# Sink column in the softmax, subtractions and sums moved to GpSimd, and three reordered places in a two-layer diffusion backbone

## The chip, the cores and the metric

The kernel runs on one core of one Trainium2 chip. The metric is device time in microseconds (us) of one execution; it is quoted as the median of several. Engines are named as in the profile: PE (TensorE matmul), PEld (its weight loads, beside PE), DVE (VectorE), ACT (ScalarE), POOL (GpSimd) and SP (SyncE, which here only issues DMAs).

## The reference

Two layers over 1024 latent tokens of width 1024, with a prefix of 256 context tokens. Layer 0 is windowed attention: 16 query heads, 4 key/value heads, head width 128. Each latent query sees the keys within 128 positions and all 256 context keys, in one softmax that also has a learned sink logit per head. Layer 1 is a convolution branch. Each branch has a SiLU gate; each layer adds gate × branch to the stream; a final RMSNorm ends it.

```python
# layer 0, per head, block of 128 queries
p = softmax(concat([sink, ctx scores, window scores (masked)]))   # the sink's own p is dropped
o = p_ctx @ v_ctx + p_win @ v_win
y = (o * silu(z)) @ w_out
# layer 1
a, gl, z = split(h @ w_in + b_in, 3)
u = depthwise_conv31(a * sigmoid(gl)) + dw_b
y = (silu(layernorm(u)) * silu(z)) @ w_out
# both: h = rmsnorm(x) * (1 + scale) + shift;  x += gate * y;  at the end rmsnorm(x, final_g)
```

## The kernel before, in words

Every product of the size of a layer is made of three matmuls. Each fp32 operand is split in a high part (type fp32r, a rounded copy, made by ACT) and a low part (full minus high, `split_lo`, a two-input subtraction on DVE or POOL); then high×high, high×low and low×high are summed in PSUM. SBUF is handed out as 45 pages of 128×1024 words and 6 half pages of 128×528.

The order of PE's instructions is the order of the program text; the other engines' orders are made by a planner that simulates the program, ready work of earlier text first. In a trace nearly all instructions carry line 88, that of a wrapper that records them, so they are told apart by the names of their tiles: `pss`, `psg` and `pso` are the three kinds of PSUM banks (`ps_s` two of 1024 columns, `ps_g` two of 512, `ps_o` two of 512).

The stages, in order of time:

1. **Start** (to about 100 us): modulation vectors, first norm, the first projections.
2. **Attention** (about 100 to 900 us). `steps` goes over 16 heads × 8 query blocks. One step issues on PE: `scores` of the *next* block (6 matmuls into an `s` bank), 12 matmuls of filler (`fill(FILL)`: the z and q projections of the next head, from a queue `fillq`), every fourth step a `pv` (probabilities × values), and the `transposes` of the *present* block's probabilities `p` (also into an `s` bank). Between the scores and the transposes of a block lies its softmax, on DVE, ACT and POOL: a masked copy with a running maximum (`mx`), a small DVE step that makes it `nmx` = min(−scale·mx, −sink), the Exp with its sum `l0`, a second small Exp for the sink (`es`), their sum, a reciprocal `ri`, and the scaling of `p` by POOL. The tile `sc` holds these five columns. After the transposes ACT makes `pthi` and DVE `ptlo` from the bank, which then is free.
   Beside these run: `rope` for q and k (two DMAs that swap halves, a product with cos on DVE, one with sin on POOL, their sum on DVE, a copy on ACT, a low part on POOL); `low_parts` (64 subtractions 128×512 on DVE that store the low parts of both output projections' weights to DRAM, `wolA` and `wolC`); and `ada_rest` (sums for the modulation vectors, on DVE, in `mask_page`). `after(...)` only orders an instruction behind an anchor on the same engine.
   In the last head the filler ends; from block `EARLY_FROM` the queue gets `early_proj`, which computes the first `EARLY_ROWS` row pairs of the output projection (two of their four token blocks each, 12 matmuls per row pair).
3. **Output projection of layer 0** (about 900 to 1074 us), `proj_attn`. Its last sub-block pushes eight `turn_in` jobs, which make the second token half of the input of layer 1 (`h2h`, `h2l`) and are taken up during the first chunks of `b_mm`.
4. **Convolution layer** (about 1074 to 1610 us). `b_mm(i, half)` multiplies weight chunk `i` with one token half. The first `2 * EARLY` = 4 chunks are run for half 0 and then again for half 1; all later ones do both halves in a row. DVE and POOL/ACT compute the 31 taps beside this; `layer_norm` follows on PE's fixed order, its mean taken from `vsum`.
5. **Output projection of layer 1** (from about 1610 us), `proj_out`. `evac1` adds the residual, sums squares, and for the second column half makes the root (`rstd_of`) and writes out the normed rows: one instruction per half that multiplies with the root `r` and the weight `fg` at once. The last three row pairs are held back so that the four token blocks end one after another.

Of the kernel before, what the change touches and what calls it, by code (L numbers as in the profile page):

```python
# [12 lines left out]
ALU = mybir.AluOpType  # L13
# [20 lines left out]
FILL = 12  # L34
DEFER = 6
EARLY = 2
EARLY_ROWS = 6
EARLY_FROM = 4
KEEP = 8
BYBLOCK = 3  # L40
ZV = (1, 4, 7)
# [52 lines left out]
def backbone_kernel(  # L94
# [428 lines left out]
               for t, n in (("dww", NJ * TAPS), ("wsum", NJ * 16))]  # L523

    anchor = []
    anchor_max = []

    def after(ins, anchor=anchor):
        if anchor:
# [50 lines left out]
    def low_parts():  # L580

        items = [(pair_rows(w, m, kk), d[m, kk]) for w, d in ((Wo, wolA), (Wp, wolC)) for m in range(2) for kk in range(NK)]
        for src, dst in items:
            raw = pg.alloc(F32, [2, 512], "low")
            SY.dma_start(out=raw, in_=src)
            yield "open"
            for b in range(2):
                hi = hp.alloc(F32R, None, "lhi")
                act(hi[:, 0:512], raw[:, b], AF.Copy)
                after(split_lo(V, raw[:, b], raw[:, b], hi[:, 0:512]), anchor_max)  # L590
                hp.free(hi)
                if b == 0:
                    yield "open"
            SY.dma_start(out=dst, in_=raw)
            pg.free(raw)
            yield "shut"
# [182 lines left out]
            PE.matmul(o, wl[:, kt], Hh[kt][:, sl], start=False, stop=kt == KT - 1)  # L779
            yield  # L780

    def rope(o, sl, dh, dl):
        qe, qs, m = (hp.alloc(F32, None, "rope") for _ in range(3))
        e, w, r = qe[:, 0:512], qs[:, 0:512], m[:, 0:512]
        act(e, o, AF.Copy)
        A.dma_start(out=w[0:64], in_=e[64:128])
        A.dma_start(out=w[64:128], in_=e[0:64])
        tt(V, r, o, cos[:, sl], ALU.mult)
        tt(G, w, w, sin[:, sl], ALU.mult)
        tt(V, r, r, w, ALU.add)  # L790
        act(dh, r, AF.Copy)
        split_lo(G, dl, r, dh)
        hp.free(qe, qs, m)
# [3 lines left out]
    def finish(kind, n, half, o, d):  # L797

        sl = slice(half * 512, half * 512 + 512)
        if kind in "kv" and half == 2:  # L800
            c = kvt[n][2]
            if kind == "k":
                act(c[:, 0], o[:, 0:CT], AF.Copy)
                split_lo(V, c[:, 1], o[:, 0:CT], c[:, 0])
                return None
        if kind in "qk":
            return rope(o, sl, d[0][:, sl], d[1][:, sl])
        if kind == "z":
            act(d[:, sl], o, AF.Tanh, scale=0.5)
            stt(d[:, sl], d[:, sl], 1.0, o, ALU.add, ALU.mult)  # L810
            return None
        w = CT if half == 2 else 512
        f = hp.alloc(F32, None, "vf")
        act(f[:, 0:w], o[:, 0:w], AF.Copy)

        def tail():
            if half == 2:
                vt_split(f, CT, *(c[:, i].rearrange("p (a b) -> p a b", b=P) for i in (2, 3)))
            else:
                vt_split(f, 512, *(t[:, half * 4:half * 4 + 4] for t in d))  # L820
            hp.free(f)

        return tail
# [69 lines left out]
    def scores(h, qb):  # L893
        g = h // 4
        q = qt[h]
        kk = kvt[g]
        c = kk[2]
        k0, k1 = max(qb - 1, 0), min(qb + 1, TB - 1)
        nw = (k1 - k0 + 1) * P
        s = ps_s()  # L900
        w0 = 512 - nw
        qsl = slice(qb * P, qb * P + P)
        ksl = slice(k0 * P, k0 * P + nw)
        for n, (a, b) in enumerate(((0, 0), (0, 1), (1, 0))):
            PE.matmul(s[:, w0:512], q[a][:, qsl], kk[b][:, ksl], start=n == 0, stop=n == 2)
            PE.matmul(s[:, 512:768], q[a][:, qsl], c[:, b], start=n == 0, stop=n == 2)
        p = pg.alloc(F32, [1024], "p")
        sc8 = small([P, 5], name="sc", bufs=6)
        mx, nmx, l0, es, ri = (sc8[:, i:i + 1] for i in range(5))
        w = nw + CT  # L910
        sc = dict(scale=1.0, scalar=-3.0e38, op0=ALU.add, op1=ALU.max, accum_out=mx)
        if qb == TB - 1:
            V.tensor_tensor_reduce(
                out=p[:, 0:w].rearrange("p (a b) -> p a b", a=2),
                in0=s[:, w0:768].rearrange("p (a b) -> p a b", a=2),
                in1=mask.rearrange("p (a b) -> p a b", a=2)[:, :, 0:256],
                **sc)
        else:
            V.tensor_tensor_reduce(out=p[:, 0:w], in0=s[:, w0:768], in1=mask[:, 640 - w:640], **sc)
        anchor_max[:] = [V.tensor_scalar(out=nmx, in0=mx, scalar1=-SCALE, scalar2=nsink[:, h:h + 1], op0=ALU.mult, op1=ALU.min)]  # L920
        act(p[:, 0:w], p[:, 0:w], AF.Exp, bias=nmx, scale=SCALE, accum_out=l0)
        act(es, sink[:, h:h + 1], AF.Exp, bias=nmx)
        tt(V, l0, l0, es, ALU.add)
        V.reciprocal(ri, l0)
        G.tensor_scalar(out=p[:, 0:w], in0=p[:, 0:w], scalar1=ri, scalar2=1.0, op0=ALU.mult, op1=ALU.mult)
        ptile[(h, qb)] = p

    def transposes(h, qb):
# [423 lines left out]

    def b_mm(i, half):
        wh, wl = wsB.need(i)
        if i < 2 * EARLY or late:
            o = ps_g()
        else:
            o = ps_og()
        sl = slice(half * 512, half * 512 + 512)
        for kt in range(KT):  # L1360
            mm3(o, wh[:, kt], wl[:, kt], H2h[(half, kt)], H2l[(half, kt)], kt == 0, kt == KT - 1)
            if kt % 2 and later and i >= EARLY:
                later.popleft()()
            if kt == 3:
                advance(2.6)
        kind, j = border[i]
        cur[0] = i
        bias = vt[:, boff[kind] + j:boff[kind] + j + 1]
        if kind == "gl":
            with tc.high_priority():  # L1370
                act(sigt[(j, half)], o, AF.Sigmoid, bias=bias)
        elif kind == "a":
            u = ubuf[j % 4]
            while any(k[0] == j - 4 for k in opened):
                advance(2.6)
            with tc.high_priority():
                stt(u[:, :, 8 + half * 256:264 + half * 256], v2(o), bias, v2(sigt[(j, half)]), ALU.add, ALU.mult)
            if j < EARLY:
                conv_unit(j, *((248, 512) if half else (0, 248)))
            elif half:  # L1380
                conv_unit(j, 0, 512 if j < JSPLIT else 256, 512)
        else:
            zs = zbuf[j % len(zbuf)][:, half]
            with tc.high_priority():
                act(zs, o, AF.Silu, bias=bias)
            if (j, half) in yready:
                tt(V if j % 8 in ZV else G, vh(j, half), vh(j, half), v2(zs), ALU.mult)
            else:
                spilled.add((j, half))
                SY.dma_start(out=zsd[j, :, sl], in_=zs)  # L1390
        late_now()
        if not late:
            advance(2.6)
# [56 lines left out]
    def evac1(s, b, acc):  # L1450
        h, m = subs[s]
        ns = slice(m * 512, m * 512 + 512)
        if b % 2 == 0:
            x2[(m, b // 2)] = pg.alloc(F32, [2, 512], "x2")
            x2["xr"] = pg.alloc(F32, [2, 512], "xr")
        if m == 0:
            x2[b] = small([P, 2], name="ssf", bufs=8)
        t, ss, xr = x2[(m, b // 2)][:, b % 2], x2[b], x2["xr"][:, b % 2]
        SY.dma_start(out=xr, in_=tok_rows(x1d, h, b)[:, ns])
        tt(V, t, acc, gbc[:, ns], ALU.mult)  # L1460
        tt(G if b % 2 and s < len(subs) - 1 else V, t, t, xr, ALU.add)
        if b % 2:
            pg.free(x2["xr"])
        junk = hp.alloc(F32, None, "junk")
        act(junk[:, 0:512], t, AF.Square, accum_out=ss[:, m:m + 1])
        hp.free(junk)
        if m == 0:
            return
        tt(V, ss[:, 0:1], ss[:, 0:1], ss[:, 1:2], ALU.add)
        r = rstd_of(ss[:, 0:1], D, 1)  # L1470
        dst = tok_rows(out[0], h, b)
        for m in range(2):
            t = x2[(m, b // 2)]
            os = slice(m * 512, m * 512 + 512)
            stt(t[:, b % 2], t[:, b % 2], r, fg[:, os], ALU.mult, ALU.mult)
            SY.dma_start(out=dst[:, os], in_=t[:, b % 2])
            if b % 2:
                used.append(t)
# [82 lines left out]

    run(projA)
    pg.free(*gbc0)
    for i in range(2 * EARLY):
        b_mm(i, 0)
        wsB.load()
        wsB.split()
        wsB.load()
    for i in range(2 * EARLY):
        b_mm(i, 1)  # L1570
        wsB.done(i)
        wsB.load()
    for i in range(2 * EARLY, len(border)):
        if i == len(border) - 1:
            next(projB)
        wsB.need(i)
# [67 lines left out]
```

## Time and profile before

| | |
|---|---|
| runs | 1801.05, 1803.62, 1809.96 us; median 1803.62 |
| span of the profiled execution | 1802.8 us, first to last instruction, 0.8 below the median |
| PE busy | 1731.8 us (96%) |
| DVE / ACT / POOL busy | 1245.8 (69%) / 880.4 (49%) / 797.4 us (44%) |
| mean granted TensorE clock | 0.987 |

Read first that PE is busy nearly all the time, and then where it is not: the idle time before PE's instructions, by what ended it, and the stretch after its last matmul. The busy shares of the other engines matter only where one of them is late for PE.

### The profile page before, as it was taken

To read this page: it belongs to the slowest core of one execution; us is meant where nothing else is said; L and a number is where in the kernel's file an instruction comes from. 1 tells how busy PE (TensorE), PEld (TensorE's weight loads), DVE (VectorE), ACT (ScalarE), POOL (GpSimd) and SP (SyncE) were. 2 spreads that over 40 slices of the span, in tenths; PEclk is the share of its full clock that TensorE was granted. 3 is DMA by queue.
4 is the path that set the end of the run, shared out by engine and by line. 5 is a ranking of instruction groups with operands and counts; after the bars stand their busy time and mean duration, and the time that the engine had idled before them with its cause. 6 is when DMAs were issued, how large, how long until landed. Compare 5 with 4: busy or idle time off the path is not lost. (4 is left out here: it accounts for less than half of the span.)

```text
span 1802.8 us, 24003 instructions
## 1 busy us (share of the span) xinstructions
PE 1731.8 (96%) x8383; PEld 1422.6 (79%) x8383; DVE 1245.8 (69%) x2424; ACT 880.4 (49%) x1526; POOL 797.4 (44%) x618
## 2 busy tenths in 40 slices
PE   6899999999999999999999999999999999999997
PEld 3578888788888888788788887888888888788786
DVE  5757774676656774676513349999999999866823
ACT  5345543545444444444533435655656565466730
POOL 2433334243423334333100147998988789120300
PEclk8899999999999999999999999999999999999999
DMA  9323442444334443335786723111021212376881
GB/s 298 107 68 112 144 137 76 130 132 155 103 102 129 144 138 96 123 97 163 256 282 245 252 87 106 47 36 47 24 88 33 79 40 71 113 242 238 315 279 47
DMA packets 195326, 242.46 MB, mean 134 GB/s; under 512 B 11798, under 2 KB 126790, under 8 KB 195204
## 3 DMA queue, kind: packets, MB, share of 16 engines
q1 hardware_dynamic: 188516, 230.10, 38.8%
q10 hardware_dynamic: 6688, 10.83, 2.5%
q8 instruction: 66, 1.08, 0.3%
q14 instruction: 56, 0.46, 0.1%
HBM read 188.70 MB, written 41.69 MB: 128 GB/s over the span
## 5 line engine op out<-in xcount | busy, mean ns | idle before, releaser
L88 POOL TENSOR_TENSOR odd_half<-odd_half,prod_half 128x513 f32<-128x513 f32 (+2 forms) x252 | 317.9, 1269 | 20.5 <-ACT prod_half L88 7.0
L88 POOL TENSOR_SCALAR p_page<-p_page,sc 128x640 f32<-128x640 f32 (+1 forms) x128 | 104.3, 815 | 313.4 <-DVE sc L88 191.8
L88 PE MATMUL psg<-hh_page,whi_page 128*128 128x512 f32 x600 | 238.1, 397 | 0.0
L88 PE MATMUL psg<-hh_page,wlo_page 128*128 128x512 f32 x600 | 236.9, 395 | 0.0
L88 PE MATMUL psg<-hl_page,whi_page 128*128 128x512 f32 x600 | 236.8, 395 | 0.0
L88 POOL TENSOR_TENSOR wlo_page<-wraw_page,whi_page 128x1024 fp32r<-128x1024 f32 x72 | 176.8, 2458 | 114.0 <-ACT whi_page L88 77.1
L88 ACT ACTIVATE prod_half<-ubuf,dww 128x513 f32<-128x513 f32 (+2 forms) x252 | 164.8, 674 | 108.0 <-POOL odd_half L88 104.1
L88 PE MATMUL psg<-h2l_page,whi_page 128*128 128x512 f32 x456 | 180.4, 396 | 1.8 <-DVE h2l_page L88 1.8
L88 PE MATMUL psg<-h2h_page,whi_page 128*128 128x512 f32 x456 | 181.6, 398 | 0.0
L88 PE MATMUL psg<-h2h_page,wlo_page 128*128 128x512 f32 x456 | 180.1, 395 | 0.0
L88 DVE SCALAR_TENSOR_TENSOR pss<-ubuf,wsum,pss 128x512 f32<-128x512 f32 (+3 forms) x270 | 172.6, 673 | 0.3
L88 ACT ACTIVATE p_page<-p_page,sc 128x640 f32<-128x640 f32 (+1 forms) x128 | 102.5, 801 | 143.7 <-DVE sc L88 135.5
L88 DVE SCALAR_TENSOR_TENSOR pss<-ubuf,dww,pss 128x512 f32<-128x512 f32 (+3 forms) x270 | 172.4, 673 | 0.3
L88 PEld LDWEIGHTS psg<-hh_page,wlo_page 128*128 128x128 f32 x600 | 113.0, 188 | 26.5
L88 ACT ACTIVATE pthi<-pss 128x640 fp32r<-128x640 f32 (+1 forms) x144 | 88.2, 613 | 87.6 <-PE pss L88 77.8
L88 PEld LDWEIGHTS psg<-hh_page,whi_page 128*128 128x128 f32 x600 | 113.1, 189 | 20.8 <-DVE kvc_page L88 0.4
L88 PEld LDWEIGHTS psg<-hl_page,whi_page 128*128 128x128 f32 x600 | 113.0, 188 | 20.4
L88 ACT ACTIVATE whi_page<-wraw_page 128x1024 fp32r<-128x1024 f32 x88 | 92.8, 1054 | 71.0 <-PE psg L88 23.7
L88 DVE TENSOR_TENSOR ptlo<-pss,pthi 128x640 fp32r<-128x640 f32 (+1 forms) x144 | 103.0, 716 | 31.7 <-ACT pthi L88 31.0
L88 PE MATMUL pso<-h2h_page,wlo_page 128*128 128x512 f32 x312 | 123.0, 394 | 0.0
L88 PE MATMUL pso<-h2h_page,whi_page 128*128 128x512 f32 x312 | 122.8, 394 | 0.0
L88 PE MATMUL pso<-h2l_page,whi_page 128*128 128x512 f32 x312 | 122.7, 393 | 0.0
(234 smaller groups left out, 4103.6 us busy)
## 6 DMA issues: line engine op xcount, KB each, us to landing
wraw_page<-in_conv_w_in_dram SPq DMA_DIRECT2D x48, 512.0 KB, 3.9
wraw_page<-in_attn_w_in_dram SPq DMA_DIRECT2D x40, 512.0 KB, 4.3
wo_page<-in_attn_w_out_dram SPq DMA_DIRECT2D x32, 512.0 KB, 5.3
wol_page<-wolA SPq DMA_DIRECT2D x32, 512.0 KB, 5.6
wo_page<-in_conv_w_out_dram SPq DMA_DIRECT2D x32, 512.0 KB, 7.3
wol_page<-wolC SPq DMA_DIRECT2D x32, 512.0 KB, 6.7
rope_half<-rope_half ACTq DMA_DIRECT2D x80, 128.0 KB, 3.1
araw_page<-in_ada_w_dram SPq DMA_DIRECT2D x32, 256.0 KB, 5.8
```

What stands on the lines that cost most here:

```text
L88: r = f(*a, **k)
```

## The change

- **Softmax.** The masked copy now multiplies by −SCALE and keeps the running *minimum*, started at −sink, so that it yields `nmx` itself. POOL writes −sink into column `w` of `p`, and the Exp runs over `w + 1` columns with scale −1, so that its sum holds the sink's term. The small DVE step, the small Exp and the DVE sum are gone; `sc` has three columns.
- **Low parts** of the output weights are subtracted on POOL in place of DVE, ordered behind the last scaling of `p`.
- **Query rope sums** (heads 1 to 15) are made on POOL in place of DVE.
- **`EARLY_ROWS`** 6 to 7 and **`EARLY_FROM`** 4 to 3: seven row pairs of the output projection in the filler, queued one step earlier.
- **`FIRST`** = 5 chunks of the convolution's input projection are run for half 0 before half 1, in place of 4.
- **Final norm.** The weight `fg` is multiplied in before the root is made (on POOL for the first column half except in the last sub-block, else on DVE); then the root, on ACT for the first column half and on DVE for the second.

```diff
+FIRST = 5
-EARLY_ROWS = 6
-EARLY_FROM = 4
+EARLY_ROWS = 7
+EARLY_FROM = 3
...
-                after(split_lo(V, raw[:, b], raw[:, b], hi[:, 0:512]), anchor_max)
+                after(split_lo(G, raw[:, b], raw[:, b], hi[:, 0:512]), anchor_scale)
...
-    def rope(o, sl, dh, dl):
+    def rope(o, sl, dh, dl, eng):
...
         tt(G, w, w, sin[:, sl], ALU.mult)
-        tt(V, r, r, w, ALU.add)
+        tt(eng, r, r, w, ALU.add)
...
-            return rope(o, sl, d[0][:, sl], d[1][:, sl])
+            return rope(o, sl, d[0][:, sl], d[1][:, sl], G if kind == "q" and n else V)
...
-        mx, nmx, l0, es, ri = (sc8[:, i:i + 1] for i in range(5))
+        nmx, l0, ri = (sc8[:, i:i + 1] for i in range(3))
         w = nw + CT
-        sc = dict(scale=1.0, scalar=-3.0e38, op0=ALU.add, op1=ALU.max, accum_out=mx)
+        G.tensor_copy(p[:, w:w + 1], nsink[:, h:h + 1])
+        sc = dict(scale=-SCALE, scalar=nsink[:, h:h + 1], op0=ALU.add, op1=ALU.min, accum_out=nmx)
...
-        anchor_max[:] = [V.tensor_scalar(out=nmx, in0=mx, scalar1=-SCALE, scalar2=nsink[:, h:h + 1], op0=ALU.mult, op1=ALU.min)]
-        act(p[:, 0:w], p[:, 0:w], AF.Exp, bias=nmx, scale=SCALE, accum_out=l0)
-        act(es, sink[:, h:h + 1], AF.Exp, bias=nmx)
-        tt(V, l0, l0, es, ALU.add)
+        act(p[:, 0:w + 1], p[:, 0:w + 1], AF.Exp, bias=nmx, scale=-1.0, accum_out=l0)
         V.reciprocal(ri, l0)
-        G.tensor_scalar(out=p[:, 0:w], in0=p[:, 0:w], scalar1=ri, scalar2=1.0, op0=ALU.mult, op1=ALU.mult)
+        anchor_scale[:] = [G.tensor_scalar(out=p[:, 0:w], in0=p[:, 0:w], scalar1=ri, scalar2=1.0, op0=ALU.mult, op1=ALU.mult)]
...
-        if i < 2 * EARLY or late:
+        if i < FIRST or late:
...
-        tt(V, ss[:, 0:1], ss[:, 0:1], ss[:, 1:2], ALU.add)
-        r = rstd_of(ss[:, 0:1], D, 1)
         dst = tok_rows(out[0], h, b)
         for m in range(2):
             t = x2[(m, b // 2)]
+            tt(V if m or s == len(subs) - 1 else G, t[:, b % 2], t[:, b % 2], fg[:, m * 512:m * 512 + 512], ALU.mult)
+        tt(V, ss[:, 0:1], ss[:, 0:1], ss[:, 1:2], ALU.add)
+        r = rstd_of(ss[:, 0:1], D, 1)
+        for m in range(2):
+            t = x2[(m, b // 2)]
             os = slice(m * 512, m * 512 + 512)
-            stt(t[:, b % 2], t[:, b % 2], r, fg[:, os], ALU.mult, ALU.mult)
+            if m:
+                V.tensor_scalar(out=t[:, b % 2], in0=t[:, b % 2], scalar1=r, scalar2=None, op0=ALU.mult)
+            else:
+                act(t[:, b % 2], t[:, b % 2], AF.Copy, scale=r)
             SY.dma_start(out=dst[:, os], in_=t[:, b % 2])
...
-    for i in range(2 * EARLY):
+    for i in range(FIRST):        # the two loops over the first chunks, and the start of the loop behind them
```

More of the change, by code (lines that the diff above doesn't have):

```diff
@@ L525, in backbone_kernel @@
     anchor = []
-    anchor_max = []
+    anchor_scale = []
     def after(ins, anchor=anchor):
@@ L907, in scores @@
         p = pg.alloc(F32, [1024], "p")
-        sc8 = small([P, 5], name="sc", bufs=6)
-        mx, nmx, l0, es, ri = (sc8[:, i:i + 1] for i in range(5))
+        sc8 = small([P, 3], name="sc", bufs=6)
+        nmx, l0, ri = (sc8[:, i:i + 1] for i in range(3))
         w = nw + CT
-        sc = dict(scale=1.0, scalar=-3.0e38, op0=ALU.add, op1=ALU.max, accum_out=mx)
+        G.tensor_copy(p[:, w:w + 1], nsink[:, h:h + 1])
+        sc = dict(scale=-SCALE, scalar=nsink[:, h:h + 1], op0=ALU.add, op1=ALU.min, accum_out=nmx)
         if qb == TB - 1:
-            V.tensor_tensor_reduce(
+            ttr = V.tensor_tensor_reduce(
                 out=p[:, 0:w].rearrange("p (a b) -> p a b", a=2),
@@ L918, in scores @@
         else:
-            V.tensor_tensor_reduce(out=p[:, 0:w], in0=s[:, w0:768], in1=mask[:, 640 - w:640], **sc)
-        anchor_max[:] = [V.tensor_scalar(out=nmx, in0=mx, scalar1=-SCALE, scalar2=nsink[:, h:h + 1], op0=ALU.mult, op1=ALU.min)]
-        act(p[:, 0:w], p[:, 0:w], AF.Exp, bias=nmx, scale=SCALE, accum_out=l0)
-        act(es, sink[:, h:h + 1], AF.Exp, bias=nmx)
-        tt(V, l0, l0, es, ALU.add)
+            ttr = V.tensor_tensor_reduce(out=p[:, 0:w], in0=s[:, w0:768], in1=mask[:, 640 - w:640], **sc)
+        act(p[:, 0:w + 1], p[:, 0:w + 1], AF.Exp, bias=nmx, scale=-1.0, accum_out=l0)
         V.reciprocal(ri, l0)
-        G.tensor_scalar(out=p[:, 0:w], in0=p[:, 0:w], scalar1=ri, scalar2=1.0, op0=ALU.mult, op1=ALU.mult)
+        anchor_scale[:] = [G.tensor_scalar(out=p[:, 0:w], in0=p[:, 0:w], scalar1=ri, scalar2=1.0, op0=ALU.mult, op1=ALU.mult)]
         ptile[(h, qb)] = p
@@ L1568, in backbone_kernel @@
         wsB.load()
-    for i in range(2 * EARLY):
+    for i in range(FIRST):
         b_mm(i, 1)
@@ L1572, in backbone_kernel @@
         wsB.load()
-    for i in range(2 * EARLY, len(border)):
+    for i in range(FIRST, len(border)):
         if i == len(border) - 1:
```

## The prediction

> **What bounds the kernel now.** I read the page's busy shares first, then PE's waits after the first 100 us, then the same by stretches of time.
>
> ```profile
> span 1802.8 us, 24003 instructions
> PE 1731.8 (96%) x8383; PEld 1422.6 (79%) x8383; DVE 1245.8 (69%) x2424; ACT 880.4 (49%) x1526; POOL 797.4 (44%) x618
> ```
>
> PE is the bound, and the change neither adds nor removes a matmul. It can gain only where PE idles. PE's waits after 100 us (total, times, longest):
>
> ```profile
> PE pss L88 <- POOL p_page L88: 7.5, 10, 1.8
> PE pss L88 <- DVE sc L88: 5.9, 5, 3.5
> PE pso L88 <- DVE ptlo L88: 4.6, 6, 1.7
> PE pss L88 <- DVE ptlo L88: 3.5, 3, 1.7
> PE pss L88 <- ACT qh_page L88: 2.7, 1, 2.7
> ...
> PE pss L88 <- POOL ql_page L88: 1.8, 3, 0.6
> PE psg L88 <- DVE h2l_page L88: 1.8, 2, 1.4
> ...
> PE pso L88 <- DVE vsum_page L88: 0.9, 1, 0.9
> ```
>
> The reader is to see many short waits: the transposes for `p` (10 of 128 steps), an `s` bank that DVE had not yet emptied (the rows that name sc and ptlo), a query that came late, and one place at the start of the convolution (h2l). The stretches (PE, PEld, DVE, ACT and POOL busy, PE's clock, DMA) are attention, the convolution, and the end behind the last matmul:
>
> ```profile
> 100.00:900.00 800.00, 769.71 (x4186) 655.63 (x4185) 524.31 (x1196) 379.00 (x783) 296.37 (x253) 1.00 0.42 129
> 1098.00:1546.00 448.00, 447.27 (x1922) 362.03 (x1922) 429.16 (x674) 253.45 (x354) 379.29 (x277) 1.00 0.18 55
> 1792.57:1802.80 10.23, 0.00 (x1) 0.00 (x0) 5.72 (x18) 0.93 (x3) 0.00 (x0) 0.60 0.42 146
> ```
>
> So 800.0 − 769.7 = 30.3 us of idle lie in attention, under 1 in the convolution, 10.2 at the end. That is all there is to win, besides the clock.
>
> **Softmax, low parts, rope sums: what moves.** The groups by tile (count | busy, mean ns):
>
> ```profile
> L88 DVE TENSOR_TENSOR low_page<-low_page,lhi_half 128x512 f32<-128x512 f32 x64 | 55.5, 867 | 0.0
> L88 DVE SCALAR_TENSOR_TENSOR mask_page<-wsum_raw,cs,mask_page 128x256 f32<-128x256 f32 x64 | 48.8, 763 | 0.1
> ...
> L88 DVE TENSOR_TENSOR rope_half<-rope_half,rope_half 128x512 f32<-128x512 f32 x40 | 37.5, 937 | 35.2 <-POOL rope_half L88 35.2
> ...
> L88 DVE TENSOR_TENSOR sc<-sc 128x1 f32<-128x1 f32 x128 | 28.2, 220 | 71.1 <-ACT sc L88 70.6
> L88 DVE TENSOR_SCALAR sc<-sc,nsink 128x1 f32<-128x1 f32 x128 | 26.6, 208 | 0.9
> ```
>
> ```profile
> L88 POOL TENSOR_TENSOR rope_half<-rope_half,sin_page 128x512 f32<-128x512 f32 x40 | 52.6, 1316 | 79.6 <-DMA rope_half<-rope_half 77.6 <-DVE sc L88 2.0
> ...
> L88 POOL MEMSET ubuf<- 128x16 f32 x8 | 0.5, 108 | 8.4 <-PE pso L88 8.4
> ```
>
> ```profile
> L88 ACT ACTIVATE sc<-sink,sc 128x1 f32<-128x1 f32 x128 | 35.8, 280 | 0.0
> ```
>
> DVE loses 55.5 (all low parts) + 30 × 0.94 = 28.1 (query sums: 15 heads × 2 halves) + 26.6 + 28.2 = 138 us of its 524 in attention. ACT loses 35.8. POOL gains 94 two-input operations of 128×512 at 1.32 = 124 us (the product with sin is the same shape), and 128 one-column copies. No row has such a copy; between nothing and a two-input operation (1.32), it is nearest to the memset of 16 columns, so 0.11 each, 14 us. POOL goes from 296 to 434 of 800 us, 54%.
>
> In the chain from scores to transposes three links go: 0.21 + 0.28 + 0.22 = 0.7 us per step. What may come back is POOL: the scaling of `p` stands in its queue behind a low part or a query sum (1.3 each), and the Exp now waits for a copy that POOL issues. The copy needs only a free page, so it can run while the scores are made; without that cover ACT, and behind it `pthi`, waits up to 1.3. The anchor puts the low parts behind a scaling and ahead of the next, a step of 800/128 = 6 us later on the mean. The masked copy now needs the sink column at its start; that is made once, before the first step.
>
> The low parts' stores wait in SP's queue for POOL in place of DVE:
>
> ```profile
> SPq L88 <- DVE low_page L88: 56.0, 27, 5.2
> ```
>
> SP stood 2.1 us a time there, with loads behind it. POOL's 1.32 in place of 0.87 makes it 2.5. What is behind are weight chunks a head ahead and the sums' inputs; no PE wait above names a load, so I put nothing on it, and if that cover went, 27 × 0.4 = 11 us of later loads would be shared out over 27 places.
>
> *Transposes that wait for `p`:* 10 waits, 7.5 us. Bounds: all 7.5 gone, since the 0.7 covers most waits of 0.75 mean; or 3 us lost, if two or three steps per rope half newly wait for POOL. I take 4.0, half way and a little above, as only 10 of 128 steps waited at all.
>
> *Banks that DVE empties late:* 4.6 + 3.5 by ptlo, and 5.9 − 3.5 = 2.4 by sc without the longest, 10.5 us. DVE has 26% less work there, and 71 + 35 us of standing in its queue for ACT and POOL shrink too. Bounds: 0 (ACT's `pthi` is late instead) and 9. I take 4.5.
>
> *Queries that come late:* 2.7 + 1.8 in four waits. The sum takes 1.32 on POOL in place of 0.94, and POOL's product with sin already waits for DMAs (77.6 us in the row above). Lost: 4 × 0.4 = 1.5. Bounds: 1 gained (no hop to DVE and back) and 4 lost.
>
> **The contention of DVE with POOL.** The same kind of row by shortest, median and longest ns:
>
> ```profile
> L88 DVE TENSOR_TENSOR low_page<-low_page,lhi_half x64: 671/681/2125, 163.3 to 796.5; 128x512 f32<-128x512 f32 x64
> ```
> ```profile
> L88 DVE SCALAR_TENSOR_TENSOR mask_page<-wsum_raw,cs,mask_page x64: 469/478/2631, 114.2 to 860.9; 128x256 f32<-128x256 f32 x64
> ```
>
> DVE operations with two inputs in SBUF are at times stretched by 1 to 2 us, about one POOL operation. The low parts lose 64 × (867 − 681) = 12 us by it, the sums in `mask_page` 64 × (763 − 478) = 18 us. The first go; the second stay, and with POOL busier by 434/296 they lose some 8 us more. That is inside the 138 that DVE is rid of.
>
> The Trainium skill ("SBUF — State Buffer", section "Who interferes with whom") says that a DVE instruction with two SBUF inputs contends with a GpSimd instruction that reads SBUF, and whichever issued first holds the port while the other blocks. The stretched rows agree. By that rule alone 94 more holders on GpSimd speak against the change, and the terms for `p` and the banks would shrink; this is the first rival below.
>
> **One step earlier into the output projection.** PE around the longest wait:
>
> ```profile
> 864.66 0.28 PE L88 MATMUL pss<-kvc_page,ql_page 128*128 128x256 f32 x1
> 868.46 0.74 PE L88 MATMUL pss<-ident,p_page 128*128 128x128 f32 x5 [3.52 <-DVE sc L88]
> ...
> 870.50 0.63 PE L88 MATMUL psg<-woh_page,ozh_page 128*128 128x512 f32 x1
> 870.92 0.63 PE L88 MATMUL psg<-wol_page,ozh_page 128*128 128x512 f32 x1
> 871.35 0.63 PE L88 MATMUL psg<-woh_page,ozl_page 128*128 128x512 f32 x1
> ```
> ```profile
> 755.00:765.00 10.00, 8.43 (x37) 7.03 (x38) 5.57 (x14) 4.02 (x8) 4.51 (x4) 0.83 0.29 93
> 864.66:874.44 9.78, 6.26 (x26) 5.05 (x25) 8.43 (x16) 8.44 (x15) 2.40 (x4) 0.83 1.05 400
> 1094.00:1104.00 10.00, 8.24 (x27) 5.80 (x26) 10.00 (x21) 7.63 (x15) 9.61 (x9) 0.83 0.39 113
> ```
>
> The scores of block 4 of the last head end at 864.9 and the transposes of block 3 follow directly: the filler has run out. `EARLY_FROM` = 3 puts 12 matmuls there, at 447.27/1922 = 0.233 each (the convolution's row) 2.8 us of the 3.5. Behind the wait matmuls start 0.42 apart and the clock is 0.83 over 9.78 us: about half rate for 3.4 us, 1.7 us lost. The same follows the waits at 755 and 1098. Without the long wait this goes too. Is the first row pair ready?
>
> ```profile
> 855.20 1.23 DVE L88 TENSOR_TENSOR ozl_page<-ozf_page,ozh_page 128x1024 fp32r<-128x1024 f32 x1
> ```
>
> Its last operand is made at 855, ahead of 865. Bounds: 3.5 + 1.7 = 5.2 (the shorter softmax covers the rest of the wait), and 0, if DVE's six or seven `ozl`, moved forward by a step with their DMAs on SP, are late for the softmax there. I take 4.0. The seventh row pair only shifts 12 matmuls from behind the attention, where PE does not wait, to the queue's end: nothing, as PE is covered by the other token blocks.
>
> **Five first chunks.** Half 1 of chunk 0 needs `h2l`, which DVE makes too late (1.8 us, and the slow clock of the window at 1094, 1.7). A fifth chunk of 24 matmuls, 5.6 us, lies between: gain 3.5 at most. But the convolution's DVE is busy 429 of 448 us, and its last product, vsum, already holds PE for 0.9. What PE arrives earlier there is partly waited for: bounds 0 and 3.5, taken 2.0. The fifth chunk's weight split has the four chunks before it, 22 us, to be done in.
>
> The Trainium skill ("TensorE: Matmul & The Clock Gate", section "Part 1: The HAM clock gate") gives the drop to half rate to an idle window of about 3.4 us. The trace does not agree with that length: the longest wait for h2l is 1.4 us and half rate follows. By the rule this term would be 1.0 in place of 2.0 and the time 1790.3; the row decides.
>
> **The end.** The DVE and ACT rows behind the last matmul:
>
> ```profile
> 1794.89 1.41 DVE L88 SCALAR_TENSOR_TENSOR x_page<-x_page,r,fg_page 128x512 f32<-128x512 f32 x2
> 1796.22 0.15 DVE L88 TENSOR_SCALAR ms<-ssf 128x1 f32<-128x1 f32 x1
> ...
> 1797.66 1.41 DVE L88 SCALAR_TENSOR_TENSOR x_page<-x_page,r,fg_page 128x512 f32<-128x512 f32 x2
> ```
> ```profile
> 1794.06 0.63 ACT L88 ACTIVATE junk_half<-x_page 128x512 f32<-128x512 f32 x1 [1.52 <-DVE x_page L88]
> ```
>
> The last block's root waits for block 2's two products (1.41), and its own two (1.41) follow on DVE alone. After: the second half's weight product (1.41/2 = 0.7) can only follow the square, at 1794.8 with its readout, the first half's lies beside it; then the root's 1.6 (1.44 from its first row to the last product, and the sum ahead of it); then one product each on ACT (0.63, as the square) and DVE (0.7 at most). End at 1794.8 + 0.7 + 1.6 + 0.7 = 1797.8, against 1799.1: 1.3 gained. Bounds: 2.0 (the product inside the root's gap) and −0.7 (DVE still backed up). Block 0 to 2 pay with DVE time under PE's work.
>
> **Sum.** 4.0 + 4.5 − 1.5 + 4.0 + 2.0 + 1.3 = 14.3 us. The span of 1802.8 becomes 1788.5; the median of the runs is 0.8 above this execution, so 1789.3. All upper ends give 28 us, all lower ends a loss of 8.
>
> **The rivals.** A change of 0.5%, 9 us, is about what a measurement of this kernel can tell from none.
>
> 1. *POOL and DVE hold each other up* (the stretched rows): the terms for `p` and for the banks fall from 8.5 to 2. Then 14.3 − 6.5 = 7.8, 1796, no change. For it: POOL at 54% and in order. Against: the stretching that goes with the low parts (12 us) is more than what comes (8). Chance 0.25.
> 2. *Slower: POOL's queue at the query halves.* In each of 30 halves product, sum and low part stand one behind the other (4 us with 1.3 added), the first behind a DMA; a scaling of `p` behind them makes PE wait. If each half costs PE x, the loss is 30x; it passes the gain plus 9 at x = 0.78. At 0.9 it is 27 − 14 = 13 slower, 1816. Against: 128 steps made only 10 such waits. Chance 0.08.
> 3. *Nearly all of attention's short waits go,* with the slow clock at 755: 28 us, 1775. For it: DVE's relief is a quarter of its work. Chance 0.12.
>
> The forecast holds 0.55. Faster: 0.55 + 0.12 = 0.67; same 0.25; slower 0.08. The range goes from rival 3 to past rival 1, 1775 to 1805.
>
> **What would show it.** DVE busy in 100 to 900 falls from 524 to about 390 and POOL rises to about 434. The chain's wait at the transposes for POOL's `p` falls under 4 us; the 3.5 us wait at 868 is gone and the clock there 1.00; no wait for h2l, a larger one for vsum; the stretch behind the last matmul is about 9 us. The prediction is wrong if waits for POOL's `p`, or for `ql`, grow: then POOL, not DVE, was the link to spare.

## The result, and the profile after

The changed kernel takes 1787.4 us (median of 4 runs, 1784.3 to 1789.3) against 1803.0 us of the kernel before on the same chip: ratio 0.9895 (0.9874 to 0.9916), 1.0% faster. The forecast was 1789.3 us. The quotient of the two medians is 0.9913; here such quotients and the ratios given differ by up to 0.002, so a gap of less than some 4 us between two versions is not told apart unless their intervals are clear of each other. One of the four runs of experiment 2 below took 2839.0 us at a granted clock of 0.57, and its ratio leaves that run out. The profiled execution has a span of 1787.4 us, 15.4 less than before. The page's busy shares (wrapper line now 89):

```profile
span 1787.4 us, 23804 instructions
PE 1731.3 (97%) x8383; PEld 1428.6 (80%) x8383; DVE 1147.8 (64%) x2078; ACT 866.8 (48%) x1406; POOL 940.5 (53%) x844
```

PE's waits after the first 130 us (releaser; total, times, longest), the whole list; one more, near 125 us for `rope_half`, stood at 1.9 us before and stands at 2.8:

```profile
PE pss L89 <- ACT qh_page L89: 10.8, 3, 3.9
PE pss L89 <- POOL ql_page L89: 3.2, 3, 2.4
PE pso L89 <- DVE vsum_page L89: 1.5, 1, 1.5
PE psg L89 <- DVE rope_half L89: 0.9, 1, 0.9
PE pso L89 <- DVE mask_page L89: 0.3, 1, 0.3
```

Every row that the forecast wanted gone is gone: POOL's `p` (7.5), `ptlo` (8.1), `sc` (5.9), `h2l` (1.8). But two rows that stood at 4.5 together now stand at 14.0: the query's high and low part. The stretches (PE, PEld, DVE, ACT and POOL busy, PE's clock, DMA):

```profile
100.00:900.00 800.00, 781.70 (x4229) 670.70 (x4228) 427.57 (x847) 362.58 (x656) 433.02 (x475) 0.98 0.43 132
345.00:360.00 15.00, 10.98 (x42) 8.69 (x41) 4.56 (x8) 6.15 (x11) 12.22 (x12) 0.77 0.30 96
...
748.00:763.00 15.00, 9.76 (x35) 7.94 (x36) 3.11 (x7) 4.61 (x9) 9.16 (x10) 0.66 0.28 89
862.00:872.00 10.00, 10.00 (x59) 8.93 (x58) 5.79 (x9) 7.32 (x10) 1.60 (x2) 1.00 1.04 402
1085.00:1095.00 10.00, 10.00 (x45) 8.11 (x44) 10.00 (x20) 8.35 (x17) 9.53 (x10) 1.00 0.32 90
1777.64:1787.40 9.76, 0.40 (x2) 0.00 (x0) 4.49 (x16) 2.26 (x5) 0.00 (x0) 0.67 0.39 135
```

POOL stands at 433 us in attention (forecast 434), DVE at 428 (forecast 390). The stretch at 862, where the 3.5 us hole was, and the start of the convolution at 1085 have a full PE and a full clock. The last row is the end, here from the start of the last matmul: 9.76, where the kernel before took 10.64 (from the matmul's end 9.35 and 10.24; forecast about 9). In the second and third rows, 15 us around 351 and 751, PE does 11.0 and 9.8 us of work, at 0.77 and 0.66 of the clock; around 551 it does 10.6 at 0.77. At the last of the three places there was a smaller stop before, of 2.7 us; the other two are new.

The hole, in PE's rows: the output projection's matmuls now stand ahead of the transposes, which wait for nothing.

```profile
863.11 0.39 PE L89 MATMUL psg<-woh_page,ozl_page 128*128 128x512 f32 x1
863.34 0.71 PE L89 MATMUL pss<-ident,p_page 128*128 128x128 f32 x5
```

The groups (count | busy, mean ns of one | idle before, by what):

```profile
L89 POOL TENSOR_TENSOR low_page<-low_page,lhi_half 128x512 f32<-128x512 f32 x64 | 83.5, 1305 | 0.0
...
L89 POOL COPY p_page<-nsink 128x1 f32<-128x1 f32 x128 | 26.6, 216 | 86.3 <-PE pss L89 22.3 <-PE psg L89 20.5 <-DMA wolA<-low_page 12.6
...
L89 DVE SCALAR_TENSOR_TENSOR mask_page<-wsum_raw,cs,mask_page 128x256 f32<-128x256 f32 x64 | 50.2, 785 | 0.1
```

A low part costs 1.305 us on POOL (put at 1.32), the one-column copy 0.216, twice the 0.11 estimated from the memset. The sums in `mask_page` went only from 763 to 785 ns: of the contention that rival 1 feared, little shows here.

Now the new wait. The first half of head 5's query, in POOL's rows and in ACT's:

```profile
344.12 1.29 POOL L89 TENSOR_TENSOR rope_half<-rope_half,sin_page 128x512 f32<-128x512 f32 x1 [2.79 <-DMA rope_half<-rope_half]
345.39 0.70 POOL L89 TENSOR_SCALAR p_page<-p_page,sc 128x512 f32<-128x512 f32 x1
346.05 1.29 POOL L89 TENSOR_TENSOR low_page<-low_page,lhi_half 128x512 f32<-128x512 f32 x1
347.30 1.44 POOL L89 TENSOR_TENSOR rope_half<-rope_half,rope_half 128x512 f32<-128x512 f32 x1
```
```profile
348.65 0.63 ACT L89 ACTIVATE lhi_half<-low_page 128x512 fp32r<-128x512 f32 x1 [3.28 <-DMA low_page<-in_attn_w_out_dram]
349.19 0.58 ACT L89 ACTIVATE rope_half<-psg 128x512 f32<-128x512 f32 x1
349.67 1.05 ACT L89 ACTIVATE whi_page<-wraw_page 128x1024 fp32r<-128x1024 f32 x1
...
350.61 0.62 ACT L89 ACTIVATE qh_page<-rope_half 128x512 fp32r<-128x512 f32 x1
```
```profile
351.28 0.58 PE L89 MATMUL pss<-kh_page,qh_page 128*128 128x256 f32 x1 [3.86 <-ACT qh_page L89]
```

On POOL, a scaling and a weight's low part stand between the query's product and its sum; the sum ends at 348.74; straight behind the product it would have ended at 345.41 + 1.44 = 346.85. On ACT three more instructions, one of which had waited for a DMA, come ahead of the copy to `qh`. From ACT's copy of the projection to the `qh` copy the half took 11.0 us here and 6.1 before. PE has only the 24 matmuls of the other half between this half's projection and the scores. Heads 5, 9 and 13 are the three of 15 queries for which that is so: the first query that is projected after a new group's key and value has no filler behind it.

### The profile page after: what moved, and what is told of

Same layout as the page of the kernel before. It is cut to its first block, busy times and chain, and to the rows that moved or that the text cites. A ratio compares the mean times of both kernels' runs of the same rounds, so it can differ in the third digit from the quotient of the medians.

```text
span 1787.4 us, 23804 instructions
## 1 busy us (share of the span) xinstructions
PE 1731.3 (97%) x8383; PEld 1428.6 (80%) x8383; DVE 1147.8 (64%) x2078; ACT 866.8 (48%) x1406; POOL 940.5 (53%) x844
## 4 chain that ended last, share of the span: by engine, by line
PE 91%; DMA 3%; DVE 2%; issue 1%; ACT 1%; POOL 1%; SPq 0%; ACTq 0%; POOLq 0%; DVEq 0%
PE psg L89 46%; PE pss L89 23%; PE pso L89 21%; DMA rope_half<-rope_half 1%; DMA low_page<-in_conv_w_out_dram 1%; DVE alo_page L89 1%; SPq L89 0%; DMA araw_page<-in_ada_w_dram 0%; DMA ozd<-oz_half 0%; DVE ptlo L89 0%; DMA ozf_page<-ozd 0%; DMA x_page<-in_x_dram 0%; POOL ql_page L89 0%; DMA low_page<-in_attn_w_out_dram 0%; DVE hf_page L89 0%
## 5 line engine op out<-in xcount | busy, mean ns | idle before, releaser
L89 POOL TENSOR_TENSOR odd_half<-odd_half,prod_half 128x513 f32<-128x513 f32 (+2 forms) x252 | 313.4, 1252 | 24.1 <-ACT prod_half L89 10.9
L89 ACT ACTIVATE p_page<-p_page,sc 128x641 f32<-128x641 f32 (+1 forms) x128 | 102.9, 804 | 96.9 <-DVE sc L89 91.6
L89 PEld LDWEIGHTS psg<-hh_page,whi_page 128*128 128x128 f32 x600 | 114.8, 191 | 21.6 <-DVE kvc_page L89 0.7
```

The lines of the kernel that those rows point to most:

```text
L89: r = f(*a, **k)
```

## The experiments

Each edit is against the changed kernel; each time is compared with the kernel before on the same chip. Theory A says that the sum on POOL makes the three queries late and that this costs a good part of the gain; the rivals are named in each expectation.

**1. All query sums back on DVE.**

```diff
-            return rope(o, sl, d[0][:, sl], d[1][:, sl], G if kind == "q" and n else V)
+            return rope(o, sl, d[0][:, sl], d[1][:, sl], V)
```

> The changed kernel with all query rope sums back on DVE; all else as changed. What it tests: in the changed kernel PE waits 14.0 us for queries (ACT qh 10.8 in 3, POOL ql 3.2 in 3), at the first block of heads 5, 9 and 13, where before it waited 4.5. Theory A, the sum on POOL makes the query late: its 1.44 us in place of 0.68, and a low part of 1.3 us that stands between product and sum in POOL's queue. Then these waits fall back to 4 to 6 us and half rate of the clock behind them goes with them: 8 to 14 us faster than the changed kernel, about 1773 to 1779. Theory B, it is the order of ACT's queue (the high copy of the query stands behind a copy that waits for a DMA): the waits stay above 9 us and the time is 1783 to 1788. DVE gets 28 us of work back; if the short waits for p and for the banks come back with it, up to 5 us are lost again.

1775.7 us, ratio 0.9841 (0.9821 to 0.9862): 11.7 us less than the changed kernel (10 by the ratios). Its PE waits:

```profile
PE pss L89 <- POOL ql_page L89: 3.3, 3, 1.1
PE pss L89 <- DVE sc L89: 2.1, 4, 1.1
...
PE pss L89 <- ACT qh_page L89: 1.2, 1, 1.2
PE pss L89 <- DVE ptlo L89: 0.9, 2, 0.7
```

The wait for `qh` falls from 10.8 to 1.2, and behind 130 us no stretch of attention has a lowered clock. Theory A holds: the sum's place on POOL made these queries late. The run does not part the two delays that hang on it, the work ahead of the sum on POOL and ACT's order behind it, about 1.9 us each at head 5; both are gone. DVE pays with 3.0 us at the banks (sc, ptlo).

**2. The three queries' ropes first in the planner.**

```diff
+        if kind == "q" and n in (5, 9, 13):
+            with tc.high_priority():
+                return rope(o, sl, d[0][:, sl], d[1][:, sl], G)
```

> The changed kernel with the rope of queries 5, 9 and 13 given high priority in the planner, so that its steps stand ahead of other ready work in the queues of ACT, DVE and POOL; PE's order and the engines are unchanged. Theory A (the longer sum itself): the sum still takes 1.4, so 1 to 3 us gained, 1784 to 1787. Theory B (what stands ahead of it in the queues): at 351 the query's copy came 11.6 us after the projection's, of which 1.3 was a low part on POOL and 1.9 ACT's queue, so the waits fall from 14 to under 6 us and the half rate goes: 8 to 14 us gained, 1773 to 1779.

1787.6 us, ratio 0.9905 (0.9874 to 0.9937). The order of instructions on PE, DVE, ACT and POOL was that of the changed kernel, and the waits nearly so (`qh` 10.6): the edit tests nothing and serves as a repeat.

**3. Two more filler matmuls a step in heads 4, 8 and 12.**

```diff
-            fill(FILL)
+            n = FILL
+            if h and h % 4 == 0 and qb < 6:
+                n += 2
+            elif (12, 5) < (h, qb) < (14, 2):
+                n -= 1
+            fill(n)
```

> The changed kernel with 2 more filler matmuls in each of the first six steps of heads 4, 8 and 12 (12 in all, given back behind head 12 by one fewer in 12 steps), so that the projections of queries 5, 9 and 13 are ready one step earlier on PE. No engine's work changes. Theory C: these three are the only queries that end right ahead of their first scores, because the step at the group's boundary has no filler; one step (4 us) of lead is more than the 4.0 us that the longest of the three waits lasts. Then the waits for queries all but go: 14 us of waits and the half rate behind them, some 15 to 22 us gained, 1766 to 1772. If A or B alone were the cause and the lead is eaten by the queues, less than 6 us.

1792.3 us, ratio 0.9936 (0.9911 to 0.996): slower than the changed kernel by 4.9 us, with intervals that touch, and far from the 15 to 22 us of gain that theory C promised. The design failed: the scores come forward as far as the projection, so still only 24 filler matmuls lie between them. At heads 5 and 9 the wait for `qh` is gone, but `ql` holds PE there for 2.2 and 2.3 us, and block 2 of the same heads waits for `sc` (4.3 together). Head 13 waits 6.3 us for `qh`, and heads 14 and 15, which were on time in the changed kernel, 1.9 and 1.3.

**4. Low parts back on DVE.**

```diff
-                after(split_lo(G, raw[:, b], raw[:, b], hi[:, 0:512]), anchor_scale)
+                after(split_lo(V, raw[:, b], raw[:, b], hi[:, 0:512]), anchor_max)
...
+        anchor_max[:] = [ttr]
```

> The changed kernel with the low parts of the output weights back on DVE, ordered behind the masked copy as before. Relief theory (DVE freed of 55 us is what ended the waits for banks and p): DVE busy in 100 to 900 goes from 428 to about 483, and 4 to 8 us of short waits for p, sc and ptlo come back: 1791 to 1795, less what the queries gain because no low part stands between product and sum on POOL. Chain theory (the 0.7 us shorter softmax ended the waits): waits for p and banks stay under 2 us and the time is 1782 to 1788.

1783.1 us, ratio 0.9877 (0.9853 to 0.99). Its PE waits and its low parts:

```profile
PE pss L89 <- DVE ptlo L89: 4.3, 6, 0.9
PE pso L89 <- DVE ptlo L89: 3.1, 2, 1.5
PE pss L89 <- ACT qh_page L89: 2.5, 3, 1.9
...
PE pss L89 <- POOL p_page L89: 0.5, 2, 0.3
```
```profile
L89 DVE TENSOR_TENSOR low_page<-low_page,lhi_half 128x512 f32<-128x512 f32 x64 | 66.1, 1032 | 0.3 <-ACT lhi_half L89 0.3
```

Two things come apart here. The waits for banks return (7.4 us; 8.1 before): it was the low parts that made DVE late for them. The wait for `p` does not (0.5): that one went with the softmax. And with the sum still on POOL but no low part between product and sum, the queries are late by 4.0 (2.5 + 1.5) in place of 14.0. From ACT's copy to `qh` the first halves of heads 5, 9 and 13 take 7.4, 7.0 and 8.5 us here, 11.0, 10.5 and 9.8 in the changed kernel and 6.1, 5.8 and 8.6 before: most of the delay is the low part that stood ahead of the sum, with what follows from it on ACT, and little is the slower sum behind a scaling. So this version is even the faster one by the medians (the intervals overlap), though a low part on DVE takes 1.03 us in place of 0.87 before. Whether low parts on POOL are worth anything once these queries are on time was not run.

**5. The old softmax, all else changed.**

```diff
-        G.tensor_copy(p[:, w:w + 1], nsink[:, h:h + 1])
-        sc = dict(scale=-SCALE, scalar=nsink[:, h:h + 1], op0=ALU.add, op1=ALU.min, accum_out=nmx)
+        sc = dict(scale=1.0, scalar=-3.0e38, op0=ALU.add, op1=ALU.max, accum_out=mx)
+        V.tensor_scalar(out=nmx, in0=mx, scalar1=-SCALE, scalar2=nsink[:, h:h + 1], op0=ALU.mult, op1=ALU.min)
+        act(p[:, 0:w], p[:, 0:w], AF.Exp, bias=nmx, scale=SCALE, accum_out=l0)
+        act(es, sink[:, h:h + 1], AF.Exp, bias=nmx)
+        tt(V, l0, l0, es, ALU.add)
```

> The changed kernel with the softmax of before (running maximum, its own step for nmx, a second Exp for the sink and the DVE sum); low parts, rope sums and the three reordered places as changed. Chain theory (the three links gone are what ended the waits of the transposes for p): PE's waits for POOL's p come back, 4 to 8 us in total, and with them a few of the banks: 1792 to 1798. Relief theory (DVE freed of the low parts and sums is enough): waits for p stay under 2 us and the time is within 3 us of the changed kernel, 1785 to 1790, as POOL is rid of 27 us of copies.

1799.0 us (10 runs), ratio 0.9973 (0.9955 to 0.9991): the softmax is worth 11.6 us (14 by the ratios), the largest gain of the parts undone here. Its PE waits, in the slowest of the ten runs (1803.5):

```profile
PE pss L89 <- POOL p_page L89: 9.5, 7, 3.3
PE pss L89 <- POOL ql_page L89: 6.1, 3, 2.2
PE pss L89 <- ACT qh_page L89: 4.3, 2, 3.7
```

The wait for `p` is back, and larger than the 7.5 before, with more in POOL's queue. From PE's next instruction behind the scores to the scaled `p` a step took 6.0 us on the mean of 128 before, 4.4 after and 6.15 here; 16, none and 16 transposes start within 0.3 us of the scaling. The link saved was worth not 0.7 us a step, as the three rows add up to, but 1.6. The rows tell where it lay. Between the masked copy and the Exp, where the small DVE step stood, passed 1.28 us on the mean before (0.29 at the shortest) and 0.32 after (0.04); between the Exp and the reciprocal, where the small Exp and the DVE sum stood, 0.92 (0.50) and 0.35 (0.12). The shortest passages differ by 0.6 together, the means by 1.5: the other 0.9 is time that the links stood behind other work on DVE and ACT.

**6. Only the sums of queries 1, 5, 9 and 13 on DVE.**

```diff
-            return rope(o, sl, d[0][:, sl], d[1][:, sl], G if kind == "q" and n else V)
+            return rope(o, sl, d[0][:, sl], d[1][:, sl], G if kind == "q" and n % 4 != 1 and n else V)
```

> The changed kernel with the rope sums of queries 1, 5, 9 and 13 alone on DVE (8 of the 30 halves); PE's order is the same. Theory A, at these three boundaries POOL's queue between product and sum makes the query late and nothing else of the 30 sums on POOL costs PE anything: the waits for the query's high copy fall from 10.8 to under 2.5 and the half rate behind them goes, as with all sums on DVE (1775.7): 1773 to 1778. If the other 22 sums on POOL cost something too, for instance through the contention of the two engines, it stays 3 us or more above 1775.7.

1771.7 us, ratio 0.9813 (0.9781 to 0.9844), 4 us under the 1775.7 with all sums on DVE (the intervals overlap). So the other 22 halves on POOL cost nothing that shows; what is left of the query waits:

```profile
PE pss L89 <- POOL ql_page L89: 3.7, 3, 1.5
...
PE pss L89 <- ACT qh_page L89: 1.2, 1, 1.2
```

**7. All sums on DVE and a true lead** for heads 5, 9 and 13: 12 filler matmuls more are issued behind the query's projection, drawn from the steps that follow.

```diff
-            return rope(o, sl, d[0][:, sl], d[1][:, sl], G if kind == "q" and n else V)
+            return rope(o, sl, d[0][:, sl], d[1][:, sl], V)
...
+            if h and h % 4 == 0:
+                fill(12)
...
-            fill(FILL)
+            n = FILL
+            if h and h % 4 == 0 and qb < 6:
+                n += 2
+            elif (12, 7) < (h, qb) < (14, 4):
+                n -= 1
+            fill(n)
```

> All rope sums on DVE, and a true lead for queries 5, 9 and 13: 12 filler matmuls more ahead of the first scores of these heads (2 more in each of six steps, so that the query's projection ends earlier, and 12 of the next projection placed between its end and the scores; given back behind head 12 by one fewer in 12 steps). In the run with extra filler alone the scores came forward by as much as the projection, 72 and 96 matmuls into the head, so there was no lead. Theory C, what is left of the wait at these heads (1.3, 1.3 and 2.6 us with all sums on DVE) is lead on PE: it goes, 4 to 6 us below 1775.7, 1769 to 1772. If the planner's new order of the queues moves other waits in its place, no gain or a loss of up to 8 us.

1773.2 us, ratio 0.9818 (0.9787 to 0.9849), against 1775.7 without the lead, a gap that the overlapping intervals do not confirm. The waits for `qh` and `ql` fall from 4.5 to 2.1 together, but those for `ptlo` (2.3 for 0.9), `vf` (1.3 for 0.7) and `r` (1.3 for none) grow. A lead does serve the query; other waits take most of it back.

**8. The three places undone:** the early row pairs, the first chunks and the final norm as before, the softmax and POOL's work as changed.

```diff
-FIRST = 5
-EARLY_ROWS = 7
-EARLY_FROM = 3
+FIRST = 4
+EARLY_ROWS = 6
+EARLY_FROM = 4
...
-            tt(V if m or s == len(subs) - 1 else G, t[:, b % 2], t[:, b % 2], fg[:, m * 512:m * 512 + 512], ALU.mult)
...
-            if m:
-                V.tensor_scalar(out=t[:, b % 2], in0=t[:, b % 2], scalar1=r, scalar2=None, op0=ALU.mult)
-            else:
-                act(t[:, b % 2], t[:, b % 2], AF.Copy, scale=r)
+            stt(t[:, b % 2], t[:, b % 2], r, fg[:, os], ALU.mult, ALU.mult)
```

> The changed kernel with the three reordered places undone together, which lie in different stretches of the trace: 6 early row pairs from block 4, 4 first chunks, final norm as before. Each is read from its own stretch. Early row pairs: the wait at the transposes of block 3 of the last head comes back, 1 to 3.5 us (DVE is less late there than before), with half rate for 3.4 us if it is over some 2 us. First chunks: PE waits again for h2l, 1.4 to 1.8 us and half rate behind it, and the wait for vsum goes from 1.5 back to about 0.9. Final norm: the stretch behind the last matmul goes from 9.7 to 10.6 us. In all 5 to 9 us slower than the changed kernel, 1792 to 1796.

1795.9 us (10 runs), ratio 0.9944 (0.9927 to 0.9962), 8.5 more than the changed kernel; the three terms had been put at 4.0 + 2.0 + 1.3 = 7.3. Waits and stretches:

```profile
PE pss L89 <- DVE sc L89: 3.6, 1, 3.6
...
PE psg L89 <- DVE h2l_page L89: 1.8, 2, 1.4
...
PE pso L89 <- DVE vsum_page L89: 0.9, 1, 0.9
```
```profile
857.00:867.00 10.00, 8.56 (x33) 7.46 (x34) 7.38 (x12) 6.39 (x10) 3.27 (x5) 0.66 0.97 365
1085.00:1095.00 10.00, 8.22 (x27) 5.84 (x26) 10.00 (x21) 7.42 (x15) 9.61 (x9) 0.83 0.39 110
1782.96:1793.60 10.64, 0.40 (x2) 0.00 (x0) 5.79 (x20) 1.13 (x4) 0.00 (x0) 0.61 0.42 149
```

Each of the three stands again where it stood: the hole with its slow clock (3.6, and 6.8 us at half clock), the wait for `h2l`, and 10.64 us behind the start of the last matmul against 9.76. vsum goes back from 1.5 to 0.9, as forecast.

**9. Sums and low parts of queries 1, 5, 9 and 13 on DVE.**

```diff
-    def rope(o, sl, dh, dl, eng):
+    def rope(o, sl, dh, dl, eng, lo=G):
...
-        split_lo(G, dl, r, dh)
+        split_lo(lo, dl, r, dh)
...
+            return rope(o, sl, d[0][:, sl], d[1][:, sl], G if kind == "q" and n % 4 != 1 and n else V,
+                        V if kind == "q" and n % 4 == 1 else G)
```

> The changed kernel with the rope sums and the low parts of queries 1, 5, 9 and 13 on DVE (PE's order unchanged). With the sums alone there (1771.7) PE still waited 3.7 us in three times for the low parts of these queries, which POOL makes behind a low part of the weights or a scaling. If POOL's queue is what makes them late, these waits fall to under 1 us: 2 to 4 us below 1771.7, 1768 to 1770. If DVE is as late, no gain, 1771 to 1774.

1768.3 us (1766.7 to 1770.1), ratio 0.9801 (0.9785 to 0.9816): 19 us faster than the changed kernel (17 by the ratios), by an edit of eight halves, and the fastest of all versions here. Its PE waits behind 130 us (two of 0.3 left out), and its attention:

```profile
PE pso L89 <- DVE vsum_page L89: 1.5, 1, 1.5
PE pss L89 <- DVE ql_page L89: 1.3, 3, 0.6
PE pss L89 <- ACT qh_page L89: 1.2, 1, 1.2
PE psg L89 <- DVE rope_half L89: 0.4, 1, 0.4
...
```
```profile
100.00:900.00 800.00, 793.45 (x4334) 680.60 (x4333) 447.06 (x875) 370.08 (x668) 418.02 (x461) 1.00 0.45 141
```

PE idles 6.6 of 800 us there, against 18.3 after and 30.3 before.

**10 and 11. The lead of 7, on 6 and on 9.**

> The rope sums of queries 1, 5, 9 and 13 on DVE, the other 22 halves on POOL, with the true lead of 12 matmuls for queries 5, 9 and 13. With all sums on DVE the lead took the three waits from 5.2 to 2.1 and moved others in; here DVE is rid of 21 us more, so the waits for banks that the lead's run had (ptlo 2.3, sc 2.3) should halve: 1768 to 1772. If the planner's order decides, it stays within 2 us of 1773.

> Both: sums and low parts of queries 1, 5, 9 and 13 on DVE, and the lead of 12 matmuls. If lateness in POOL's queue and lack of lead on PE are two separate parts of the wait, all waits for queries behind the first 130 us go and the time is 1765 to 1769. If one covers the other, it is the same as the better of the two alone.

1773.6 us (ratio 0.9829, 0.9814 to 0.9843) and 1771.5 us (0.9816, 0.98 to 0.9833), not better than 1771.7 and 1768.3 without it. In both, waits for `sc` (2.8 and 2.2) and smaller ones come in. Head 13 stays late all the same: 2.0 us for `ql` in 10 and 2.8 for `qh` in 11, each with half clock behind it, where 11 was to have no query wait left. This lead is of no use once DVE makes these queries.

## Why the prediction was right, and which of its terms were not

The total came out at 1787.4 for 1789.3, but so close a number is luck: two large errors in attention offset each other. Of the signs that the prediction named for being wrong one came true: PE's wait for `ql` grew, from 1.8 to 3.2, and with it that for `qh`, from 2.7 to 10.8. For three queries POOL was indeed the link to spare. PE's matmuls up to the last head have the same order before, after and in experiment 9, which there hardly waits. So the starts of the same scores, counted from the first ones and set against experiment 9, show what each kernel loses, the waits too short for a row and the slowed clock included. Up to the scores that start at 854 in the trace after:

| lost against experiment 9, us | before | after |
|---|---|---|
| around the first scores of head 5 | 0.0 (346.72 to 358.22) | 6.5 (340.36 to 358.35) |
| of head 9 | 0.0 (546.63 to 558.25) | 6.9 (540.60 to 559.09) |
| of head 13 | 3.3 (746.16 to 762.17) | 7.2 (740.65 to 760.59) |
| everywhere else | 23.0 | 1.4 |
| sum | 26.3 | 22.0 |

(In brackets: the scores ahead of the late ones, to those behind them; in experiment 9 the three stretches take 11.5, 11.6 and 12.7 us. Of the 1.4 after, nearly all is lost near 125 us, where the clock fell in this profile and not in that of experiment 9.)

- *Transposes and banks:* right in kind, far too small. 4.0 + 4.5 = 8.5 was taken, the upper bounds gave 16.5, and 21.6 came (23.0 − 1.4). All four rows of waits went, and with them waits that no row lists. Experiments 4 and 5 show whose work it was: the low parts' for the banks, the softmax's for `p`. The 0.7 us a step was the wrong measure of a chain whose links stood behind other work on DVE and ACT; it became 1.6 shorter.
- *Queries:* the step that failed. Taken −1.5, bounds +1 to −4; it was −17.3. The working priced the longer instruction (four late queries, 0.4 each; even that was low, as the 0.94 is a mean with the keys' sums and a query's sum mostly took 0.68) and not the place in the queue: a scaling and a low part in front of the sum on POOL, and with the sum later, ACT's planned order behind it. About 9.5 of it are the waits (14.0 − 4.5); the rest goes with the lowered clock at each of them, which held for 6.8, 6.8 and 10.2 us, against 3.4 once before. Rival 2 had named this place, POOL's queue at the query halves, but as a cost of every half; it is a cost of three queries, those whose scores come next. The other queries have slack: experiment 6 leaves 22 halves on POOL at no cost that shows.
- *The hole:* 4.0 taken. From those scores to the last product with the values, 5.7 us were gained, the 12 matmuls brought forward (2.8) counted as work done. The wait is gone and the clock at 1.00; `ozl` was not late. The excess over the bound of 5.2 is short waits of the last blocks.
- *Five first chunks:* 2.0 taken, 3.8 found from the first product of the convolution to vsum (481.5 us before, 477.7 after). PE's wait for vsum grew from 0.9 to 1.5, as forecast, but only by 0.6: what was "partly waited for" was little.
- *End:* 1.3 taken, 0.9 found from the start of the last matmul. In DVE's rows the weight product of the second half comes after the square, and the root behind it, as worked out:

```profile
1780.28 0.69 DVE L89 TENSOR_TENSOR x_page<-x_page,fg_page 128x512 f32<-128x512 f32 x1
...
1782.53 0.49 DVE L89 TENSOR_SCALAR x_page<-x_page,r 128x512 f32<-128x512 f32 x1
```

- Another 1.0 us came from a wait for `r` in the layer norm, not forecast. It is back in experiments 3, 5, 6, 7, 8 and 10 and gone in 1, 2, 4, 9 and 11, so it goes with no one part of the change; the planner's order is the likely cause, which was not shown.
- *Contention* (rival 1): about 5 us on DVE for the 8 put (1.4 in the row of `mask_page` above, 3.6 in the 48 other sums of that tile, 652 to 728 ns), with no trace of it in PE's waits.
- *DVE's relief:* its busy time in attention fell by 97 us and not by 138. The rows themselves fell by 117: the 30 query sums had taken 0.73 each and not 0.94 (6 us), the masked copy grew by 8 and the work in `mask_page` by 7. The other 20 us are rows that overlap at their ends, so that the sum of the rows is more than the busy time. The 26% less work behind the term for the banks was 18%.
- *The low parts' stores:* SP stood 4.3 us a time for POOL (72.7 in 17) and not 2.5. No wait of PE names a load, so the nothing that was put on it stands.

By stretches: start −0.3, attention 21.6 − 17.3 + 5.7 = 10.0, convolution 3.8, then 1.0, and 0.9 at the end: 15.4. What stays open is why the planner put the low part ahead of the query's sum in these places; experiment 2 was meant to turn it round and did not.

## What to carry to other kernels

Moving work to a slower engine that works through its queue in order was free here where the result had slack and dear where it was the next thing that the bound engine needed. So don't price a move by instruction time × count: list for each instance what stands in the new queue between its input and it, and how much work of the bound engine lies between its output and the use. Here 22 of 30 moved halves cost nothing that shows, the six of heads 5, 9 and 13 cost 17 us (the two of head 1 were not tried alone), and keeping eight sums on the old engine made a change of 1.0% into one of 1.9%, or 2.0% with these queries' low parts on DVE as well.

## What the hardware showed

- Half clock came with waits much shorter than the 3.5 us of the hole: with PE waits of 1.4 us (for `h2l`, one of 0.4 just ahead of it) and of 1.2 and 1.1 us close together (experiment 6), up to 6.3 us (for `qh`, experiment 3), and held for 3.4 to 10.2 us. At one place, near 125 us, waits of 2.7 to 3.0 us brought it in eight of these profiles and not in three (experiments 4, 7 and 9), so the length of the wait alone does not decide it. The Trainium skill ("TensorE: Matmul & The Clock Gate", section "Part 1: The HAM clock gate") gives an idle window of about 3.4 us; these waits do not agree with that length.
- The masked copy took 877 ns in its new form (a minimum with the start value read from a column), against 817 in the old one (a maximum with a constant); both are means beside other work, and which part of the new form costs was not tried:

```profile
L89 DVE CUSTOM_DVE_ANT_0 p_page<-pss,mask_page,nsink 128x640 f32<-128x640 f32 x96 | 84.2, 877 | 14.4 <-PE pss L89 13.3
```

- The same DVE low part took 0.87 us on the mean before, with POOL busy for 296 of 800 us, and 1.03 with the query sums on POOL (experiment 4, 359 of 800). Its median is 0.68 and 0.69, so what grows is the few that are stretched.
